# The front of an encoder trunk as one list of steps: no low parts on GpSimd, six chunks of h made by ScalarE, early transposes of the identity

## The chip, the cores and the metric

The kernel runs on one core of one Trainium2 chip. The metric is the time of one execution on the device, in microseconds (us). An execution has five engines that take their instructions in order and signal each other by semaphores: TensorE (PE, with its weight loads PEld), VectorE (DVE), ScalarE (ACT), GpSimd (POOL) and SyncE (SP, which here only issues transfers). The profile is of one profiled execution.

## The reference

One layer of a trunk over two inputs (prompt and sample, 512 rows of 1024 each). What matters here is its beginning, for the first input:

```python
c_act = jax.nn.silu(c)
mod = c_act @ w_ada[l] + b_ada[l]
sh1, sc1, g1, sh2, sc2, g2 = [m[:, None, :] for m in jnp.split(mod, N_MOD, axis=-1)]
h = rms_norm(x, norm1_g[l]) * (1.0 + sc1) + sh1
proj = h @ w_in[l]
q_a, k_a, v_a, q_r, k_r, v_r, g_r = jnp.split(proj, IN_OFFSETS, axis=-1)
```

Behind it come windowed attention on `q_a, k_a, v_a` (768 columns of `proj`), bidirectional retention on the rest, an output projection, a second norm and a squared-ReLU MLP, and a final norm. Everything is float32.

## The kernel before

**Products.** A float32 product is made of three matmuls of the type fp32r. Each operand is split in a high part (a cast, usually on ACT) and a low part (the value less its high part, a subtraction on DVE or POOL); `mm3` then adds high by high, high by low and low by high in one PSUM bank.

**The front.** The first 83 us work on the prompt alone. The 1024 inner columns are cut into eight chunks `kc` of 128. For each chunk the kernel needs: `xT[kc]`, the normed rows of x, transposed (`px`, PE, from four tiles of x that DVE has scaled by their own root mean square); a shift and a scale per column, `mod_s` and `mod_a`, from 128 columns of `w_ada` each; `hm = xT*a + s` (L326, DVE), its high part (L327, ACT) and low part (L328, DVE); and 768 columns of `w_in` (`wi`), split in `wih` and `wil`. `products(kc, ...)` multiplies the chunk into six open banks, `first`, one for each 128 columns of k, v and the four pieces of q: 18 matmuls of 512 columns a chunk. When chunk 7 is through, the banks are read and the retention and attention stages start.

**The modulation.** Chunk 0 and 1 have their columns of `w_ada` loaded alone (`one`: two halves of the 1024 rows, 512 bytes a run), the others by pairs of chunks (`pair`: for the scale, s=1, and the shift, s=0, two halves each of 512 KB). A pair's half is split (`wh_ada` on ACT, L97; `wl_ada` on DVE for half 0 and on POOL for half 1, L1002), 16 matmuls with the four columns `c4` give a row `pm`, ACT copies it out (`mr`, L221), two transposes turn it into columns (`pmt`, L229), and DVE adds their parts and finishes `mod` (L232, L234, L202, L204).

**What sets the order.** The front is written by hand as a program; `pin` makes every engine keep that order, up to chunk 6. Instructions of later stages are not pinned and may be put between pinned ones. Transfers that SP issues go one after another through one queue: where one waits for a buffer, all behind it wait. Raw tiles of `w_in` from chunk 2 on, and all later raw weights, share three buffers (`raw`); most other tiles share 32 buffers (`r4`). A raw tile's buffer comes free when its low part is made, which is on POOL for chunks 0 to 6 (L1025). The split parts of the chunks are also written to DRAM (`kept_first`, ACT's queue, L1048) for the second input, which reads them back around 207 to 250 us.

Of the kernel before, what the change touches and what calls it, by code (L numbers as in the profile page):

```python
# [15 lines left out]
P = 128  # L16
# [14 lines left out]
def trunk_kernel(ctx, tc, x0, x1, c0, c1, w_ada, b_ada, norm1_g, w_in, attn_sink, decay_f, decay_b,  # L31
# [123 lines left out]
    nc.gpsimd.dma_start(dec[:, 0, :], decay_f.broadcast_to([P, RH]))  # L155
    nc.gpsimd.dma_start(dec[:, 1, :], decay_b.broadcast_to([P, RH]))
    sink = const.tile([P, AH], F32, name="sink")
    nc.gpsimd.dma_start(sink, attn_sink.broadcast_to([P, AH]))
# [8 lines left out]

    def conditioning():
        ps = aux_bank("ps_rows")
        nc.tensor.transpose(ps[:, :80], rows, ident[:80, :80])  # L170
        nc.vector.tensor_copy(cols, ps[:, :80])
        th = small([P, 16], "cth")
        nc.scalar.activation(th, cols[:, 0:16], AF.Tanh, scale=0.5)
        yield
        nc.vector.scalar_tensor_tensor(cact.rearrange("p k b -> p b k"), th.rearrange("p (b k) -> p b k", b=NB), 1.0,
                                       cols[:, 0:16].rearrange("p (b k) -> p b k", b=NB), ALU.add, ALU.mult)
        nc.vector.tensor_scalar(cact, cact, 0.5, None, ALU.mult)
        yield
        nc.vector.tensor_scalar(onep, bcol[:, KC:2 * KC], 1.0, None, ALU.add)
        nc.vector.tensor_copy(c4[:, :, 0:2], cact)  # L180
        nc.vector.tensor_sub(c4[:, :, 2:4], cact, f(c4[:, :, 0:2]))
        yield
# [23 lines left out]
    def ada_sums(name, ws, done, stops=(), paired=False):  # L206

        split = isinstance(ws[0], list)
        m = 4 if split else NB
        pm = aux_bank(f"pm_{name}")  # L210
        out = pm[:m, :256].rearrange("p (c n) -> p c n", c=2)
        for kk in range(KC):
            kh, k = divmod(kk, 4)
            sides = [(c4, w) for w in ws[kh]] if split else [(cact, ws[kh].rearrange("p (c k n) -> p c k n", c=2, n=P))]
            for s, (c_, w) in enumerate(sides):
                nc.tensor.matmul(out, c_[:, kk, :], w[:, :, k, :], start=(kk == 0 and s == 0),
                                 stop=(kk == KC - 1 and s == len(sides) - 1))
            if kk in stops:
                yield
        mr = small([4, 256], f"mr_{name}", tag="mr", bufs=2)  # L220
        nc.scalar.copy(mr[:m, :], pm[:m, :256])  # L221
        yield
        pt = aux_bank(f"pmt_{name}")
        for c in range(2):
            mc = mr[:m, c * P:(c + 1) * P]
            if paired:
                nc.tensor.matmul(pt[:, c * 2:c * 2 + 2], mc, pairing, start=True, stop=True)
            else:
                nc.tensor.transpose(pt[:, c * m:c * m + m], mc, ident[:m, :m])  # L229
        if split and not paired:  # L230
            m4 = small([P, 2, 4], f"m4_{name}")
            nc.vector.tensor_copy(m4.rearrange("p c s -> p (c s)"), pt[:, 0:8])  # L232
            ms = small([P, 2, 2], f"ms_{name}")
            nc.vector.tensor_tensor(ms, m4[:, :, 0:2], m4[:, :, 2:4], ALU.add)  # L234
        else:
            ms = pt[:, 0:4].rearrange("p (c b) -> p c b", c=2)
        for c in range(2):
            done(c, ms[:, c, :])
        yield
# [75 lines left out]
    def x_rstd(b, t, xt):  # L315
        ssq = small([P, 1], f"ssq_{b}_{t}")
        nc.scalar.activation(junk(f"jk_{b}_{t}"), xt, AF.Square, accum_out=ssq)
        return rms_rstd(ssq, f"x_{b}_{t}")
# [184 lines left out]
    def masked_distance():  # L503
        nc.vector.tensor_scalar(sink8, sink, 8.0, None, ALU.mult)
        di = r4f("di")
        da, dm = di[:, :384], di[:, 384:768]
        nc.vector.scalar_tensor_tensor(da, dl[:, 256:640], -1.0, dl[:, 256:640], ALU.mult, ALU.max)
        nc.vector.tensor_scalar(dm, da, 128.5, MASKED, ALU.is_gt, ALU.mult)
        nc.vector.tensor_tensor(da, da, dm, ALU.add)
        return da  # L510

    def bias_tables(da):
        for h in range(AH):
            nc.scalar.activation(bias_t[:, h, :], da, AF.Copy, scale=-8.0 * 2.0 ** -(h + 1))
            yield
# [5 lines left out]
    def log_decays():  # L521
        decf = dec.rearrange("p a h -> p (a h)")
# [451 lines left out]
    xt0 += [load_x_tile(0, t) for t in range(2, NT)]  # L974
    wi, pairs = {}, {}

    def load_wi(kc):
        wi[kc] = raw_unit(cols_unit(w_in, kc, 1, 0, 768), f"wi_{kc}", spare=kc < 2)

    def load_one(kc):  # L980
        one = []
        for kh in range(2):
            t = r4f(f"raw_ada1_{kc}_{kh}")
            for s in range(2):
                in_order(nc.sync.dma_start(t[:, s * 512:(s + 1) * 512].rearrange("p (k n) -> p k n", n=P),
                                           cols_unit(w_ada, kh * 4, 4, s * D + kc * P, P)))
            one.append(t)
        return one

    def load_pair(kc):  # L990
        for s in (1, 0):
            for kh in range(2):
                pairs[kc, s, kh] = raw_unit(cols_unit(w_ada, kh * 4, 4, s * D + kc * P, 256), f"ada1_{kc}_{s}_{kh}", True)

    def high_pair(kc, s):
        for kh in range(2):
            t = pairs[kc, s, kh]
            pairs[kc, s, kh] = t, split_high(t, f"ada1_{kc}_{s}_{kh}", spare_ws if s == 0 else None)

    def low_pair(kc, s, kh, engine):  # L1000
        t, w = pairs[kc, s, kh]
        engine.tensor_sub(w[1], t, f(w[0]))  # L1002
        pairs[kc, s, kh] = [x.rearrange("p (k c n) -> p c k n", k=4, c=2) for x in w]

    def high_one(kc, kh):
        ones[kc][kh] = ones[kc][kh], split_high(ones[kc][kh], f"ada1_{kc}_{kh}", spare_ws)

    def low_one(kc, kh, engine):
        t, w = ones[kc][kh]
        engine.tensor_sub(w[1], t, f(w[0]))  # L1010
        ones[kc][kh] = [x.rearrange("p (c k n) -> p c k n", c=2, n=P) for x in w]

    def one(kc, **kw):
        return ada_sums(f"{kc}", ones[kc], lambda c, m: first_mod(c == 1, kc, m), **kw)

    def pair(kc, s):
        return ada_sums(f"{kc}_{s}", [pairs[kc, s, kh] for kh in range(2)], lambda c, m: first_mod(s == 1, kc + c, m))

    def split_wi(kc, engine=nc.vector, low=nc.gpsimd):
        w = [r4(f"wi{s}_{kc}").rearrange("p a n -> p (a n)")[:, :768] for s in "hl"]  # L1020
        if engine is nc.scalar:
            nc.scalar.copy(w[0], wi[kc][:, :768])
        else:
            nc.vector.tensor_copy(w[0], wi[kc][:, :768])
        low.tensor_sub(w[1], wi[kc][:, :768], f(w[0]))  # L1025
        wi[kc] = w

    def take_xT(kc, pt):
        if kc % 2 == 0:
            pair = r4(f"xT_{kc}", F32)  # L1030
            xT.extend([pair[:, 0, :], pair[:, 1, :]])
        if kc % 2 == 0:
            nc.scalar.copy(xT[kc], pt)
        else:
            nc.vector.tensor_copy(xT[kc], pt)

    def prepare(kc):
        hT[0].append(modulated(0, 0, kc, xT[kc]))

    def products(kc, c0, c1):  # L1040
        w, h_ = wi[kc], hT[0][kc]
        for c in range(c0, c1):
            cs = slice(order[c] * P, (order[c] + 1) * P)
            mm3(open_banks[c], (w[0][:, cs], w[1][:, cs]), (h_[:, 0, :], h_[:, 1, :]), kc == 0, kc == KC - 1)
        if c1 == 6:
            for k in ([] if kc == 0 else [kc - 1] if kc < KC - 1 else [kc - 1, kc]):
                for s in range(2):
                    nc.scalar.dma_start(kept_first[:, :, s, k * P:(k + 1) * P],  # L1048
                                        f(wi[k][s]).rearrange("p (c n) -> p c n", n=P))
# [43 lines left out]
    for kc in range(4):  # L1093
        take_xT(kc, banks[kc])
# [409 lines left out]
```

## Time and profile before

| what | us |
|---|---|
| median of 3 runs | 1155.02 (1154.34 to 1156.5) |
| the profiled execution | 1155.35 |
| its span in the trace | 1153.5 |
| first matmul of `products` starts | 24.21 |
| last matmul of `products` starts | 82.54 |
| PE busy in the span | 1108.4 (96%) |
| DVE, ACT, POOL busy | 899.6, 497.6, 68.2 |

The span is the time between the first and the last instruction that the trace shows; the profiled execution's own time is 1.85 us longer. A row of the timeline has the start, the duration, the engine, the line, the operation and its tiles, and in brackets the idle time of the engine just before it and what ended that. A row of the windows has busy time and number of instructions for each engine in a stretch, the clock granted to TensorE as a share, the mean busy share of the 16 DMA engines (it can be above 1, where packets overlap) and the rate of transfer.

### The profile page before, as it was taken

How to read it: one execution, taken by the hardware profiler on the slowest of the kernel's cores; microseconds unless marked ns; L12 is line 12 of the kernel's file. 1: busy time of each engine (PE TensorE's matmuls, PEld its weight loads, DVE VectorE, ACT ScalarE, POOL GpSimd, SP SyncE). 2: the span in 40 equal slices, each digit the busy share in tenths (PEclk: the TensorE clock that was granted, in tenths of full speed). 3: DMA queues.
4: the chain of work that ended last, by engine and by line, in shares of the span. 5: the costliest groups of instructions: out<-in, count | busy, mean ns of one | idle time of the engine just before them, and what ended most of it. 6: DMA issues, size and time to landing. Idle time of an engine off the chain costs nothing.

```text
span 1153.5 us, 14407 instructions
## 1 busy us (share of the span) xinstructions
PE 1108.4 (96%) x5167; PEld 903.5 (78%) x5167; DVE 899.6 (78%) x1496; ACT 497.6 (43%) x847; POOL 68.2 (6%) x79
## 2 busy tenths in 40 slices
PE   5989999999999999998999999999989999999995
PEld 3668787778888878887888888888778888888884
DVE  4888988978888687699998778876659655679675
ACT  4446765435554243355333333333434542335341
POOL 3620001100000000000000000000000000000011
PEclk9999999999999999999999999999999999999999
DMA  9786677665454689950655455442793455625503
GB/s 287 243 268 223 206 233 265 221 204 172 160 178 159 194 282 325 351 185 26 210 195 179 161 169 177 170 162 103 258 356 99 147 190 183 226 84 183 183 19 145
DMA packets 125135, 224.36 MB, mean 194 GB/s; under 512 B 8500, under 2 KB 59780, under 8 KB 125064
## 3 DMA queue, kind: packets, MB, share of 16 engines
q1 hardware_dynamic: 112168, 217.14, 55.9%
q10 hardware_dynamic: 12544, 6.29, 1.9%
q8 instruction: 40, 0.66, 0.2%
q0 software_dynamic: 352, 0.03, 0.2%
q14 instruction: 31, 0.25, 0.1%
HBM read 152.36 MB, written 71.06 MB: 194 GB/s over the span
## 4 chain that ended last, share of the span: by engine, by line
PE 78%; DVE 9%; DMA 7%; ACT 2%; issue 2%; POOL 1%; POOLq 0%; SPq 0%; ACTq 0%; DVEq 0%
PE x L1326 13%; PE px_None L937 12%; PE y L1326 11%; PE py_None L937 9%; PE po L129 2%; PE po L130 2%; PE po L128 2%; PE po L429 1%; PE ppt L422 1%; PE psc L396 1%; PE pj_rv L128 1%; PE pj_rv L130 1%; PE pj_rv L129 1%; PE pj_rg L130 1%; PE pj_rg L128 1%
## 5 line engine op out<-in xcount | busy, mean ns | idle before, releaser
L843 DVE TENSOR_TENSOR uc_l<-ur,uc_h 128x1024 fp32r<-128x1024 f32 x56 | 68.3, 1221 | 48.2 <-ACT uc_h L842 31.2
L1326 PE MATMUL x<-wc_h,uc_h 128*128 128x512 f32 x256 | 99.9, 391 | 4.4 <-DVE acc L1367 3.7
L1326 PE MATMUL x<-wc_l,uc_h 128*128 128x512 f32 x256 | 99.7, 390 | 0.0
L1326 PE MATMUL x<-wc_h,uc_l 128*128 128x512 f32 x256 | 99.7, 389 | 0.0
L842 ACT CAST uc_h<-ur 128x1024 fp32r<-128x1024 f32 x56 | 58.8, 1050 | 74.4 <-PE x L1326 22.7
L1326 PE MATMUL y<-wc_l,uc_h 128*128 128x512 f32 x192 | 75.6, 394 | 3.5 <-DVE wc_l L843 3.5
L1326 PE MATMUL y<-wc_h,uc_l 128*128 128x512 f32 x192 | 75.3, 392 | 0.0
L1326 PE MATMUL y<-wc_h,uc_h 128*128 128x512 f32 x192 | 75.2, 392 | 0.0
L842 ACT CAST wc_h<-w 128x1024 fp32r<-128x1024 f32 x48 | 50.4, 1050 | 49.9 <-PE x L1326 19.4
L843 DVE TENSOR_TENSOR wc_l<-w,wc_h 128x1024 fp32r<-128x1024 f32 x48 | 58.5, 1219 | 6.5 <-ACT wc_h L842 4.5
L1326 PEld LDWEIGHTS x<-wc_h,uc_h 128*128 128x128 f32 x256 | 48.1, 188 | 15.6 <-DVE acc L1367 4.5
L1326 PEld LDWEIGHTS x<-wc_h,uc_l 128*128 128x128 f32 x256 | 48.1, 188 | 10.0
L1326 PEld LDWEIGHTS x<-wc_l,uc_h 128*128 128x128 f32 x256 | 48.1, 188 | 9.9
L128 PE MATMUL po<-wh_wo,ms 128*128 128x512 f32 x128 | 50.5, 397 | 1.9 <-ACT ms L761 1.9
L129 PE MATMUL po<-wl_wo,ms 128*128 128x512 f32 x128 | 49.8, 391 | 0.3 <-DVE wl_wo L103 0.3
L130 PE MATMUL po<-wh_wo,ms 128*128 128x512 f32 x128 | 49.7, 391 | 0.0
L255 DVE SCALAR_TENSOR_TENSOR adacc_c<-raw_ada_c,cact,adacc_c 128x512 f32<-128x512 f32 x56 | 39.8, 746 | 8.6 <-DMA raw_ada_c<-in_w_ada_dram 7.6
L1326 PEld LDWEIGHTS y<-wc_l,uc_h 128*128 128x128 f32 x192 | 36.4, 190 | 11.6 <-DVE wc_l L843 4.0
L842 ACT CAST wc_s4h<-raw_w 128x1024 fp32r<-128x1024 f32 x16 | 16.9, 1054 | 62.6 <-PE px_None L937 41.6
L406 ACT ACTIVATE st<-st,negm 128x256 f32<-128x256 f32 (+1 forms) x64 | 35.2, 555 | 19.4 <-DVE negm L401 19.4
L1326 PEld LDWEIGHTS y<-wc_h,uc_l 128*128 128x128 f32 x192 | 36.5, 190 | 7.5
L1326 PEld LDWEIGHTS y<-wc_h,uc_h 128*128 128x128 f32 x192 | 36.4, 189 | 7.6
(380 smaller groups left out, 3083.3 us busy)
## 6 DMA issues: line engine op xcount, KB each, us to landing
ur<-spill SPq DMA_DIRECT2D x56, 512.0 KB, 4.1
raw_w<-in_w_mlp_dram SPq DMA_DIRECT2D x32, 512.0 KB, 3.9
spill<-s SPq DMA_DIRECT2D x64, 256.0 KB, 3.7
w<-in_w_mlp_dram SPq DMA_DIRECT2D x32, 512.0 KB, 7.0
spill<-u SPq DMA_DIRECT2D x48, 256.0 KB, 2.0
raw_ada_g<-in_w_ada_dram SPq DMA_DIRECT2D x16, 512.0 KB, 4.6
raw_ada_c<-in_w_ada_dram SPq DMA_DIRECT2D x16, 512.0 KB, 4.0
raw_ada<-in_w_ada_dram SPq DMA_DIRECT2D x12, 512.0 KB, 8.8
```

The source lines that it names most:

```text
L128: nc.tensor.matmul(ps, lhs[0], rhs[0], start=start, stop=False)
L129: nc.tensor.matmul(ps, lhs[0], rhs[1], start=False, stop=False)
L130: nc.tensor.matmul(ps, lhs[1], rhs[0], start=False, stop=stop)
L255: nc.vector.scalar_tensor_tensor(acc[b], src, cb, acc[b], ALU.mult, ALU.add)
L396: nc.tensor.matmul(psc[:, :w], qs[hh][:, isl], k_[:, s, j0 * P:j1 * P], start=(s == 0), stop=(s == 1))
L406: nc.scalar.activation(st[hh][:, :w], st[hh][:, :w], AF.Exp, bias=negm[:, hh:hh + 1], scale=0.125, accum_out=den[:, hh:hh + 1])
L422: nc.tensor.transpose(pt[:, hh * P:(hh + 1) * P], st[hh][:, jj * P:(jj + 1) * P], ident)
L429: nc.tensor.matmul(po, va[:, j0 + jj, g].rearrange("p s e -> p (s e)"), pts[jj][:, s, :], start=(jj == 0 and s == 0), stop=(jj == nj - 1 a ...
L842: nc.scalar.copy(hi, src)
L843: nc.vector.tensor_sub(lo, src, f(hi))
L937: self.last = nc.tensor.matmul(bank[:, cs], x[:, k, :], y, start=first and k == 0 and i == 0, stop=last and k == 3 and i == 2, skip_group_ ...
L1326: nc.tensor.matmul(out, left[n][x][:, i, ts_], right[n][y][:, i, :], start=first and i == 0 and k == 0, stop=end and i == 1 and k == 2, sk ...
```

## The change

The whole front becomes a list of short steps, `FRONT`, that is run in order; each step issues one piece of work (`P.2.0`: chunk 2 into bank 0; `pl.4.1.0`: the low part of pair 4, scale, half 0). `pin` again makes each engine keep the order of the list.

```diff
-    xt0 = [load_x_tile(0, t) for t in range(2)]
+    xt0 = {}
...
-        in_order(nc.sync.dma_start(rows[r0:r0 + n, :], src.rearrange("(r p) -> r p", p=P)))
+        in_order(nc.scalar.dma_start(rows[r0:r0 + n, :], src.rearrange("(r p) -> r p", p=P)))
...
+    BY_SCALAR = (0, 1, 2, 3, 5, 7)
+    kept_first = tc.dram_tile((P, KC, 2, 768), F32, name="kept_first")
+    for c in range(6):
+        kept[f"in{c * P}"] = kept_first.rearrange("p k s n -> p s k n")[:, :, :, c * P:(c + 1) * P]
...
+    def low(key, kh, form):
+        t, w = halves[key][kh]
+        nc.vector.tensor_sub(w[1], t, f(w[0]))
...
+    def step_wh(kc):
+        w = [r4(f"wi{s}_{kc}").rearrange("p a n -> p (a n)")[:, :768] for s in "hl"]
+        nc.scalar.copy(w[0], wi[kc][:, :768])
...
+    def step_wl(kc):
+        t, w = wi[kc]
+        nc.vector.tensor_sub(w[1], t[:, :768], f(w[0]))
...
+        if kc in BY_SCALAR:
+            nc.scalar.activation(d[:, 0, :], xT[kc], AF.Identity, bias=mod_s[0][:, kc, 0:1], scale=mod_a[0][:, kc, 0:1])
...
+    def step_keep(kc):
+        for s in range(2):
+            nc.gpsimd.dma_start(kept_first[:, kc, s, :], f(wi[kc][s]))
+
+    def step_warm(n):
+
+        b_ = aux_bank("warm")
+        for _ in range(n):
+            nc.tensor.transpose(b_[:, :P], ident, ident)
...
+    FRONT = """
+di.0 di.1 x.0 di.2 bias.0 bias.1 x.1 bias.2 bias.3 warm.12 psr warm.14 bias.4 cols one.0.0.0 bias.5 tanh sq.0
...
+wh.6 pm.p61.0 wh.7 pl.6.0.1 pm.p61.1 wl.6 pm.p60.0 mr.p61 wl.7 pt.p61 pm.p60.1 md.p61 P.3.5 keep.3
```

In words: all low parts are on DVE, all high parts of `w_in` on ACT. ACT makes `hm` and the high part of h for chunks 0, 1, 2, 3, 5 and 7, both straight from `xT`. The row `pm` and its columns share one bank, and a matmul with `pairing` (a 4x2 matrix of ones and zeros) adds the parts, so that DVE's copy and addition (L232, L234) go for every pair. 26 transposes of the identity stand on PE ahead of the first transposes of x. The bias tables of the attention (`bias`, ACT) are made at the start instead of among the chunks. The small loads of the conditioning (`rows`) go through ACT's queue, those of the retention (`dec`, `sink`) stand behind the front's first tiles on POOL, and the writes to `kept_first` go through POOL's queue, in runs of 3 KB instead of 512 bytes; the second input then reads them in runs of 512 bytes instead of 4 KB.

The order of SP's transfers at the start, before (x are the tiles of x, `raw_ada_0` the columns of chunk 0; two rows of one half are one tile):

```order
L146 DMA x_0_84<-in_x_prompt_dram 128x1024
L146 DMA x_1_86<-in_x_prompt_dram 128x1024
L153 DMA rows<-in_c_prompt_dram 8x128
L153 DMA rows<-in_c_sample_dram 8x128
L153 DMA rows<-in_norm_g_dram 8x128 x2
L153 DMA rows<-in_b_ada_dram 48x128
L146 DMA x_2_119<-in_x_prompt_dram 128x1024
L146 DMA x_3_121<-in_x_prompt_dram 128x1024
L985 DMA raw_ada_0_0_124<-in_w_ada_dram 128x4x128 x2
L985 DMA raw_ada_0_1_127<-in_w_ada_dram 128x4x128 x2
L89 DMA raw_wi_130<-in_w_in_dram 128x768
```

The same place after the change:

```order
L147 DMA x_0_116<-in_x_prompt_dram 128x1024
L147 DMA x_1_121<-in_x_prompt_dram 128x1024
L984 DMA raw_ada_0_0_157<-in_w_ada_dram 128x4x128 x2
L984 DMA raw_ada_0_1_171<-in_w_ada_dram 128x4x128 x2
L147 DMA x_2_183<-in_x_prompt_dram 128x1024
L147 DMA x_3_206<-in_x_prompt_dram 128x1024
L984 DMA raw_ada_1_0_219<-in_w_ada_dram 128x4x128 x2
L89 DMA raw_wi_242<-in_w_in_dram 128x768
```

Chunk 0's columns of `w_ada` come before the third and fourth tile of x, and the five small loads have left the queue. The rest of the queue up to the retention's first weights keeps its order.

POOL in the front, before, behind the last tile of x (`wil` and `wl_ada` are the low parts):

```order
L306 TENSOR_TENSOR rr_x_3_208<-rv_x_3_206,neghalf 128x1
L1025 TENSOR_TENSOR wil_241<-raw_wi_130,wih_240 128x768
L1025 TENSOR_TENSOR wil_287<-raw_wi_138,wih_286 128x768
L1002 TENSOR_TENSOR wl_ada_2_1_1_294<-raw_ada_2_1_1_142,wh_ada_2_1_1_293 128x1024
L1002 TENSOR_TENSOR wl_ada_2_0_1_341<-raw_ada_2_0_1_146,wh_ada_2_0_1_340 128x1024
L1025 TENSOR_TENSOR wil_358<-raw_wi_148,wih_357 128x768
```

And after:

```order
L1024 TENSOR_TENSOR rr_x_3_264<-rv_x_3_262,neghalf 128x1
L159 DMA dec<-in_ret_decay_fwd_dram 128x4
L160 DMA dec<-in_ret_decay_bwd_dram 128x4
L161 DMA sink<-in_attn_sink_dram 128x8
L1101 DMA kept_first<-wih_269 128x768
L1101 DMA kept_first<-wil_270 128x768
L1101 DMA kept_first<-wih_338 128x768
```

Thirteen subtractions have gone from POOL; what it has in their place is three small loads and sixteen writes, each issued as soon as its own chunk is split, since nothing else stands ahead of them on POOL.

ACT near the end of the front, before (`mr_1_665` and `mr_0_711` are the rows of pair 6, `wh_rv` the high part of the retention's first weights, not pinned):

```order
L221 COPY mr_1_665<-pm_1_648 4x256
L514 ACTIVATE bias_t<-di 128x384
L1048 DMA kept_first<-wih_449 768x1x128
L1048 DMA kept_first<-wil_450 768x1x128
L1048 DMA kept_first<-wil_595 768x1x128
L221 COPY mr_0_711<-pm_0_694 4x256
L514 ACTIVATE bias_t<-di 128x384
L1048 DMA kept_first<-wih_683 768x1x128
L327 CAST h_0_6_726<-hm_0_6_727 128x512
L1048 DMA kept_first<-wil_684 768x1x128
L97 CAST wh_rv_0_845<-raw_rv_0_843 128x1024
```

And after (`mr_p_664` and `mr_p_684` are the rows of pair 6, `wih_630` and `wih_642` the high parts of chunks 6 and 7):

```order
L97 CAST wh_ada_6_0_1_623<-raw_ada_6_0_1_556 128x1024
L1060 CAST wih_630<-raw_wi_576 128x768
L1060 CAST wih_642<-raw_wi_586 128x768
L97 CAST wh_rv_0_841<-raw_rv_0_839 128x1024
L210 COPY mr_p_664<-pm_p_633 4x256
L210 COPY mr_p_684<-pm_p_655 4x256
L522 ACTIVATE lg_z<-lg_ax 128x8
L1084 ACTIVATE h_0_7_704<-xT_376,mod_s_98,mod_a_96 128x512
L1086 CAST h_0_6_693<-hm_0_6_694 128x512
```

The high parts of the last two chunks and of the retention's first weights now stand ahead of both rows of pair 6. On PE the matmul that waits for the first of these rows (`pt.p61` in the list) stands ahead of the second half of the shift's sum, of the last product of chunk 3 and of all of chunks 4 to 7.

More of the change, by code (lines that the diff above doesn't have):

```diff
@@ L166, in trunk_kernel @@
     onep = const.tile([P, KC], F32, name="onep")
[L168 to L182, printed above, removed]
     mod_a = [const.tile([P, KC, NB], F32, name=f"mod_a{i}") for i in range(2)]
@@ L230, in ada_sums @@
[L230 to L236, printed above, removed]
-        for c in range(2):
-            done(c, ms[:, c, :])
-        yield
+            out, mc = bank_[:, 256 + c * 2:258 + c * 2], mr[key][:m, c * P:(c + 1) * P]
@@ L990, in load_pair @@
[L990 to L1017, printed above, removed]
@@ L1037, in prepare @@
[L1037 to L1049, printed above, removed]
@@ L1179, in trunk_kernel @@
-    next(tables)
-    pin(start)
-    products(KC - 2, 0, 6)
-    for c in range(6):
-        products(KC - 1, c, c + 1)
-        first[c].done(open_banks[c])
+    wi, halves, sums, mr, hm, xT, banks, open_banks, ssx, rrx = {}, {}, {}, {}, {}, {}, {}, {}, {}, {}
+    order = (4, 5, 0, 1, 2, 3)
+    BY_SCALAR = (0, 1, 2, 3, 5, 7)
+    kept_first = tc.dram_tile((P, KC, 2, 768), F32, name="kept_first")
+    for c in range(6):
+        kept[f"in{c * P}"] = kept_first.rearrange("p k s n -> p s k n")[:, :, :, c * P:(c + 1) * P]
@@ new lines, in trunk_kernel @@
+P.6.4 P.6.5 keep.6 P.7.0 P.7.1 P.7.2 P.7.3 P.7.4 P.7.5 keep.7
+    """.split()
+    start = len(nc.cur_bb.bb.instructions)
+    hT_of[0].extend([None] * KC)
+    first = attn_units(hT_of[0], 0)
+    for name in FRONT:
+        kind, *args = name.split(".")
+        if name == "P.7.0":
+            pin(start)
+        steps[kind](*[int(a) if a.isdigit() else a for a in args])
+        if kind == "P" and args[0] == "7":
+            first[int(args[1])].done(open_banks[int(args[1])])
+    hT = hT_of
```

346 lines of the change are left out of this document (159 added, 187 removed).

## Prediction

> **What bounds the kernel now.** The page first, for the whole; then the windows, by stage of the front.
>
> ```profile
> PE 1108.4 (96%) x5167; PEld 903.5 (78%) x5167; DVE 899.6 (78%) x1496; ACT 497.6 (43%) x847; POOL 68.2 (6%) x79
> ```
> ```profile
> 20.30:31.40 11.10, 10.88 (x54) 6.18 (x53) 7.41 (x16) 5.06 (x9) 3.85 (x3) 1.00 1.09 358
> 31.40:37.30 5.90, 3.77 (x28) 2.29 (x27) 5.88 (x4) 4.01 (x5) 3.88 (x2) 1.00 0.64 214
> 37.30:41.40 4.10, 4.10 (x18) 2.52 (x17) 4.05 (x3) 0.79 (x2) 4.07 (x2) 0.58 0.27 67
> 41.40:60.60 19.20, 17.92 (x94) 12.97 (x93) 15.37 (x29) 7.43 (x12) 9.30 (x6) 1.00 0.76 240
> 60.60:72.00 11.40, 9.22 (x57) 6.45 (x56) 9.49 (x18) 4.51 (x8) 5.92 (x3) 1.00 0.95 273
> 72.00:83.20 11.20, 11.20 (x47) 8.34 (x46) 8.57 (x22) 5.96 (x10) 0.00 (x0) 1.00 0.97 300
> ```
>
> PE is busy nearly all the time; behind 72 us it has no gap at all, so a front that ends sooner moves everything behind it. In the front the transfers carry 358 GB/s until 31.4 us, then fall to 67 while PE waits and its clock drops to 0.58. The queue's own waits say why, and the timeline of DVE and POOL why that took so long:
>
> ```profile
> SPq L89 <- POOL wil L1025: 27.2, 4, 9.2
> ```
> ```profile
> 33.34 3.39 DVE L1002 TENSOR_TENSOR wl_ada<-raw_ada,wh_ada 128x1024 fp32r<-128x1024 f32 x1
> ```
> ```profile
> 33.24 2.41 POOL L1002 TENSOR_TENSOR wl_ada<-raw_ada,wh_ada 128x1024 fp32r<-128x1024 f32 x1 [0.37 <-ACT wh_ada L97]
> ```
>
> SP stood 27.2 us for buffers that POOL's low parts release, and a DVE subtraction that takes 1.22 us elsewhere (below) took 3.39 with POOL's beside it. The front's marks on PE, and the pitch of its matmuls:
>
> ```profile
> 24.21 0.50 PE L128 MATMUL first<-h,wih 128*128 128x512 f32 x1
> 46.01 0.28 PE L216 MATMUL pm<-wh_ada,c 128*4 128x256 f32 x1
> 47.85 0.40 PE L128 MATMUL first<-h,wih 128*128 128x512 f32 x1
> 66.08 0.28 PE L229 MATMUL pmt<-ident,mr 4*128 4x4 f32 x2 [2.10 <-ACT mr L221]
> 66.29 0.50 PE L128 MATMUL first<-h,wih 128*128 128x512 f32 x1
> 82.31 0.39 PE L129 MATMUL first<-h,wih 128*128 128x512 f32 x1
> 82.54 0.39 PE L130 MATMUL first<-h,wil 128*128 128x512 f32 x1
> ```
>
> A product matmul starts every 0.23 us (82.31 to 82.54), so a product of three takes 0.69, a pair's 16 sums take 1.84 (46.01 to 47.85), two column matmuls 0.21 (66.08 to 66.29). The front ends at 82.54 + 0.23 = 82.8.
>
> **The change, part by part.**
>
> *Low parts to DVE.* What the move costs and frees, from the groups by form:
>
> ```profile
> L1002 DVE TENSOR_TENSOR wl_ada<-raw_ada,wh_ada 128x1024 fp32r<-128x1024 f32 x6 | 9.5, 1582 | 0.9 <-ACT wh_ada L97 0.9
> L328 DVE TENSOR_TENSOR h<-hm,h 128x512 fp32r<-128x512 f32 x8 | 9.2, 1151 | 5.5 <-ACT h L327 5.5
> L202 DVE TENSOR_SCALAR mod_a<-ms,onep,cols 128x2 f32<-128x2 f32 x6 | 5.0, 871 | 0.1
> L234 DVE TENSOR_TENSOR ms<-m 128x4 f32<-128x4 f32 x6 | 4.3, 716 | 0.2
> L1024 DVE CAST wih<-raw_wi 128x768 fp32r<-128x768 f32 x7 | 3.9, 551 | 0.0
> L1010 DVE TENSOR_TENSOR wl_ada<-raw_ada,wh_ada 128x1024 fp32r<-128x1024 f32 x2 | 2.4, 1223 | 0.0
> L1025 DVE TENSOR_TENSOR wil<-raw_wi,wih 128x768 fp32r<-128x768 f32 x1 | 1.0, 959 | 0.0
> L97 ACT CAST wh_rv<-raw_rv 128x1024 fp32r<-128x1024 f32 x2 | 2.1, 1050 | 0.0
> L221 ACT COPY mr<-pm 4x256 f32<-4x256 f32 x7 | 2.5, 360 | 12.2 <-PE pm L216 12.2
> ```
>
> DVE gains 6 x 1.22 + 7 x 0.96 = 14.0 us and loses the casts of w_in (3.9), the sums `ms` (4.3) and what POOL's neighbourhood added: 6 x (1.58 - 1.22) = 2.2 on `wl_ada`, 8 x (1.15 - 0.69) = 3.7 on h (0.69 is its duration in the undisturbed row quoted further down). So DVE has no more work than before, and 41.4 to 60.6 us shows 15.37 of 19.2. ACT gains seven casts and six second activations of about 0.6, some 9 us, over a front in which it was idle half the time. Neither becomes the bound.
>
> *The start.* Before, the fourth tile of x and the row of chunk 0 came one after the other:
>
> ```profile
> 13.02 1.06 ACT L317 ACTIVATE jk<-x 128x1024 bf16<-128x1024 f32 x1 [0.18 <-DMA x<-in_x_prompt_dram]
> ```
> ```profile
> 22.96 0.55 DVE L326 TENSOR_SCALAR hm<-xT,mod_a,mod_s 128x512 f32<-128x512 f32 x1
> ```
>
> Now the columns of chunk 0 land ahead of the last tiles, so `hm` waits for x alone. The tile's squares, root, scaling, transposes and two copies are about 6 us behind its landing; with the bytes ahead unchanged (12 to 13 us) the first product starts near 20 instead of 24.2. The eight bias tables now stand ahead of the first tiles' squares and put these off by some 2 us; the wait for the fourth tile hides that, and without it those 2 us would be the price. The identity transposes lie on PE in the same wait: nothing. The small loads of `dec` and `sink` are needed only behind chunk 6, some 40 us after POOL issues them: nothing.
>
> *Transfers.* POOL no longer holds SP, so what lands when goes by bytes. The waits for low parts stay: the raw tile of chunk 5 needs the low part of chunk 2, which lands 2.9 MB ahead of it, so 8 us or more at 350 GB/s, against some 2 us for its split. If DVE fell behind by 6 us, SP would stand again. These are the transfers of the window up to 83 us, the issue of the first write on ACT's queue, and the rates in 40 slices of 2.08 us:
>
> ```profile
> raw_ada<-in_w_ada_dram SPq DMA_DIRECT2D x12, 512.0 KB, 8.8
> raw_wi<-in_w_in_dram SPq DMA_DIRECT2D x8, 384.0 KB, 5.8
> kept_first<-wih ACTq DMA_DIRECT2D x8, 384.0 KB, 4.6
> kept_first<-wil ACTq DMA_DIRECT2D x8, 384.0 KB, 6.0
> x<-in_x_prompt_dram SPq DMA_DIRECT2D x4, 512.0 KB, 4.4
> raw_ada<-in_w_ada_dram SPq DMA_DIRECT2D x8, 256.0 KB, 6.1
> ```
> ```profile
> 46.11 0.57 ACTq L1048 DMA_DIRECT2D kept_first<-wih  x1
> ```
> ```profile
> GB/s 30 316 178 135 359 339 217 348 300 352 349 348 374 372 349 350 280 24 0 154 354 326 343 311 284 262 133 184 0 106 127 338 346 346 315 185 380 350 375 218
> ```
>
> Reads to the end of the front: 2.10 (x) + 8.39 (w_ada) + 3.15 (w_in) = 13.6 MB, and 0.52 for the retention's first weights. The first of the writes (6.3 MB) began at 46 us; now each goes out when its chunk is split, from about 18 us, into the same engines. For chunks 0 to 5 that is 12 x 0.393 = 4.7 MB ahead of the last reads: 18.9 MB. Rates are bounded by the windows, 300 (72 to 83.2) and 358 (20.3 to 31.4); I take 345, the full slices' usual figure. The flow begins near 3 us (0.52 MB had landed at 4.3, the next row), so the last read lands at 3 + 18.9/0.345 = 57.8 us; bounds 55.8 and 66.
>
> ```profile
> 4.32 1.06 ACT L317 ACTIVATE jk<-x 128x1024 bf16<-128x1024 f32 x1 [2.32 <-DMA x<-in_x_prompt_dram]
> ```
>
> *The new wait at the end.* ACT's order has `wih` of chunks 6 and 7 and `wh_rv` ahead of the rows of pair 6; all three wait for those last reads, and PE's column matmul behind the row holds all products left. From 57.8: `wh_rv` 1.05, row 0.36, columns 0.21, half a sum 0.92, one product 0.69, second row and columns 0.57, 24 products x 0.69 = 16.6. Sum 20.4: the front ends at 78.2. PE would wait some 3 us there; the earlier gap brought the clock to 0.58 for 4.1 us, so (1 - 0.58) x 4.1 = 1.7 us may be added; the gap of 2.10 at 66 us cost none. I take none and keep 1.7 for the range. The Trainium skill ("TensorE: Matmul & The Clock Gate", Part 1) has the clock fall after an idle window of about 3.4 us; by that a wait of 3 us costs nothing and the sum stays; by the row it could be 79.9. The first gap, 5.90 us with 3.77 busy, was shorter than that window and cost all the same, so the row decides for the range.
>
> *Reading back.* The second input now reads `kept_first` in 512-byte runs. `raw_rq`, in such runs, and `wh_q`, in long ones, both landed in
>
> ```profile
> DMA to landing us min/median/max: 4.9/4.9/4.9
> ```
>
> and the engines have room there, so I take 0; at worst 12 loads 15% slower than 1.5 us each, 2.7 us, if none were hidden.
>
> Sum: 78.2 - 82.8 = -4.6, so 1155.35 - 4.6 = 1150.75 for the profiled execution (span 1153.5 and the 1.85 around it, which stays); the median of the runs, 1155.02, is 0.3 below that execution. I say **1150.4**.
>
> **Rivals.**
> 1. *The writes do not hold the reads.* If they come late, 14.1 MB at 345 land by 44 us and PE is the bound: 20 + 144 x 0.23 + 6 x 1.84 + 6 x 0.21 = 65.4, with some gaps 65 to 67, gain 16, **1139**. For it: only reads are urgent. Against: POOL has nothing ahead of the writes. POOL's issue of a small write, and DVE beside it:
>
> ```profile
> 191.43 0.55 POOL L292 DMA_DIRECT2D gates<-adacc_g  x1 [6.33 <-ACT adacc_g L291]
> ```
> ```profile
> 191.73 0.68 DVE L328 TENSOR_TENSOR h<-hm,h 128x512 fp32r<-128x512 f32 x1
> ```
>
> Neither is longer than elsewhere. Yet the Trainium skill ("SBUF — State Buffer", SBUF: two separate sides) says that a transfer issued from GpSimd waits for its descriptors while DVE runs an operation that uses the shared port. By it the writes would be pushed back under a DVE that is 80% busy, which here leads to this rival; these rows do not show it.
>
> 2. *The engines are slower with reads and writes mixed* (slower than before). At 300 GB/s the last read lands at 66 us and the front ends at 86.4: +3.6, **1158.6**. The point from which it decides is 18.9/(82.8 - 20.4 - 3) = 318 GB/s. For it: 273 and 300 in the two windows that had reads and writes, and a slow start (178 and 135). Against: their slices hold holes, and full ones with both have 311 to 380; the writes' runs are six times longer.
> 3. *Nothing changes* (within 0.2%): the same place at 310 to 325 GB/s, or the clock's 1.7 us and some of the reading back on top: **1154**.
>
> **How the numbers follow.** Forecast (gain 2.5 to 10 us) 0.58; rival 1 and what lies toward it (more than 10) 0.12; rival 3 0.17; rival 2 0.13. A change of 0.2%, 2.3 us, is about what a measurement of this kernel can tell from none. So faster 0.70, same 0.17, slower 0.13. The range leaves out rival 1's far half and rival 2's: 1142 to 1157.
>
> **What would show it.** Right: POOL without subtractions, no DVE subtraction of 1024 above 1.3 us; first product near 20; transfers above 320 GB/s from 10 to 55 us, with writes from 18 us on; one long wait of PE for `mr` near 54 to 59; front's end near 78. Wrong: the wait at `mr` missing with an end below 72 (rival 1), the last reads landing after 62 (rival 2), or PE gaps behind the front that were not there.

## The result and the profile after

The changed kernel takes 1148.73 us (median of 7 runs, 1146.14 to 1149.94) against 1155.02 for the kernel before in the same rounds: ratio 0.9945, 95% interval 0.993 to 0.9959. The forecast was 1150.4, in 1142 to 1157. The profiled execution took 1147.91, its span is 1145.2: 7.4 us under the one before, and 8.3 in the span. (Of the experiments below, one execution of e6, of 3343.1 us, counts in its median but not in its ratio.) The first line of its page, with the busy time of each engine:

```profile
PE 1111.3 (97%) x5205; PEld 909.7 (79%) x5205; DVE 889.1 (78%) x1484; ACT 506.8 (44%) x860; POOL 46.8 (4%) x82
```

The windows of the front, cut as before, and one more piece of its start:

```profile
20.30:31.40 11.10, 11.10 (x63) 7.79 (x62) 9.26 (x13) 10.46 (x16) 1.08 (x2) 1.00 1.03 347
31.40:37.30 5.90, 4.01 (x27) 2.90 (x27) 4.48 (x6) 3.19 (x4) 2.15 (x4) 1.00 1.08 383
37.30:41.40 4.10, 4.10 (x30) 2.85 (x30) 1.74 (x4) 1.05 (x1) 0.00 (x0) 1.00 1.02 413
41.40:60.60 19.20, 16.78 (x97) 12.38 (x96) 15.23 (x24) 14.73 (x21) 4.34 (x8) 1.00 1.00 348
60.60:72.00 11.40, 11.40 (x52) 9.40 (x51) 6.49 (x24) 3.20 (x5) 0.00 (x0) 1.00 0.96 362
72.00:83.20 11.20, 10.88 (x54) 8.80 (x53) 7.42 (x12) 7.44 (x14) 0.00 (x0) 1.00 0.01 2
```
```profile
10.00:16.00 6.00, 5.27 (x26) 3.94 (x27) 4.64 (x8) 4.91 (x10) 1.10 (x2) 0.55 1.05 329
```

The hole in the transfers (67 GB/s at 37 to 41 us) is gone; from 20 us on they run at 347 to 413 GB/s until everything has landed. The clock is whole from 16 us on, but 0.55 from 10 to 16. Now PE's marks in its timeline (in brackets the wait just before), the last being the first product behind the front:

```profile
18.68 1.53 PE L1034 MATMUL px<-ident,x 128*128 128x128 f32 x12
20.14 1.89 PE L204 MATMUL pm_o<-raw_ada,cact 128*2 128x256 f32 x8
21.96 1.09 PE L301 MATMUL px<-ident,x 128*128 128x128 f32 x8
23.19 0.50 PE L129 MATMUL first<-h,wih 128*128 128x512 f32 x1
36.62 0.60 PE L217 MATMUL pm_p<-pairing,mr_p 4*128 4x2 f32 x4 [1.89 <-ACT mr_p L210]
42.77 0.28 PE L204 MATMUL pm_p<-wh_ada,c 128*4 128x256 f32 x1 [1.18 <-ACT wh_ada L97]
44.03 0.28 PE L204 MATMUL pm_p<-wl_ada,c 128*4 128x256 f32 x1 [0.98 <-DVE wl_ada L1055]
57.11 0.60 PE L217 MATMUL pm_p<-pairing,mr_p 4*128 4x2 f32 x4
76.38 0.39 PE L129 MATMUL pj_rv<-wh_rv,h 128*128 128x512 f32 x1
```

The front ends at 76.4 instead of 82.8. The long wait that was forecast at the row of pair 6 (57.11) is not there; the waits stand at pair 4, at 36.6 and at 42.8 to 44. ACT's timeline says what these waited for, and how close the forecast's place came:

```profile
41.67 1.04 ACT L97 CAST wh_ada<-raw_ada 128x1024 fp32r<-128x1024 f32 x1 [2.99 <-DMA raw_ada<-in_w_ada_dram]
55.74 1.05 ACT L97 CAST wh_rv<-raw_rv 128x1024 fp32r<-128x1024 f32 x1 [1.01 <-DMA raw_rv<-in_w_in_dram]
56.70 0.35 ACT L210 COPY mr_p<-pm_p 4x256 f32<-4x256 f32 x1
```

The last read that PE stands for is the last half of pair 4 (ACT has it at 41.67); from 44.03 on PE runs almost without a gap. The read of rv is in ACT's hands at 55.74, against 57.8 forecast, and the row leaves ACT at 57.05, when PE had just run dry. Groups of VectorE, SP's wait, and the writes' issue on POOL (0.54 us each; first, eighth and ninth):

```profile
L1055 DVE TENSOR_TENSOR wl_ada<-raw_ada,wh_ada 128x1024 fp32r<-128x1024 f32 x14 | 16.8, 1220 | 5.6 <-ACT wh_ada L97 5.6
L1090 DVE TENSOR_TENSOR h<-hm,h 128x512 fp32r<-128x512 f32 x8 | 5.4, 689 | 1.6 <-ACT h L1084 1.0 <-ACT h L1086 0.4 <-ACT hm L1077 0.2
```
```profile
SPq L89 <- DVE wil L1065: 6.0, 3, 3.8
```
```profile
18.59 0.54 POOL L1101 DMA_DIRECT2D kept_first<-wih  x1
34.42 0.54 POOL L1101 DMA_DIRECT2D kept_first<-wil  x1 [0.22 <-issue]
46.83 0.54 POOL L1101 DMA_DIRECT2D kept_first<-wih  x1 [11.87 <-ACT mr_p L210]
```

**Where the 6.4 us of the front come from.** From 9.4 us (before, the first transposes of x; now, the end of the early ones) to the first product of rv PE waited 8.5 us before and 5.7 now: 2.8. The other 3.6 lie in busy time: of 73.4 us 64.9 before, of 67.0 us 61.3 now. Before, the clock was half up to 20.3 us (the windows' 1.00 is no evidence there: the sums before stood 0.21 us apart, 17.93 to 18.14 in PE's timeline, and 0.12 from 20.4 on), over 8.2 us of work, which cost 4.1, and again for 3.4 us at 37.4, which cost 1.7; now it is half from 10.7 to 15.4 (sums 0.21 us apart up to 15.26, 0.11 from 15.44 on), which costs 2.3. 5.8 - 2.3 = 3.5. This divides PE's time; it does not show causes. In e1, e3, e5 and e6 below the clock is whole from about 11 us on, and the first product comes at 22.9 to 23.2 all the same, so those 2.3 us cost the first product 0.3 us at most; what the longer half clock cost the kernel before is not shown. Behind the front PE's waits up to 300 us fall from 4.1 to 1.7 us; two of those that went:

```profile
124.66 0.51 PE L130 MATMUL pj_rk<-h,wl_rk 128*128 128x512 f32 x1 [0.83 <-DVE wl_rk L103]
...
246.53 0.50 PE L130 MATMUL pj_q<-h,wl_q 128*128 128x512 f32 x1 [0.79 <-DMA wl_q<-kept_first]
```

Front and waits make 8.8 us; the span fell by 8.3. The rest of the way has gains and losses that the change did not aim at: some waits are shorter, and the same wait of 2.89 us near the end brought half clock (the matmul behind it takes 0.80 us) in this execution and none before. Here before, then after:

```profile
1127.79 0.50 PE L1326 MATMUL x<-wc_h,uc_h 128*128 128x512 f32 x1 [2.89 <-DVE acc L1367]
```
```profile
1117.96 0.80 PE L1291 MATMUL x<-wc_h,uc_h 128*128 128x512 f32 x1 [2.89 <-DVE acc L1332]
```

So the front's 6.4 us and the 6.3 us between the medians agree, but not because everything else stood still.

### The profile page after: what moved, and what is told of

It reads as the page before. It is cut to its first block, busy times and chain, and to the rows that moved or that the text cites. A ratio compares the mean times of both kernels' runs of the same rounds, so it can differ in the third digit from the quotient of the medians.

```text
span 1145.2 us, 14502 instructions
## 1 busy us (share of the span) xinstructions
PE 1111.3 (97%) x5205; PEld 909.7 (79%) x5205; DVE 889.1 (78%) x1484; ACT 506.8 (44%) x860; POOL 46.8 (4%) x82
## 4 chain that ended last, share of the span: by engine, by line
PE 81%; DVE 8%; DMA 6%; ACT 2%; issue 2%; POOL 1%; SPq 0%; ACTq 0%; POOLq 0%; DVEq 0%
PE x L1291 13%; PE px_None L933 12%; PE y L1291 12%; PE py_None L933 9%; PE po L130 2%; PE po L131 2%; PE po L129 2%; PE po L421 2%; PE ppt L414 2%; PE psc L388 1%; DMA raw_ada<-in_w_ada_dram 1%; PE pj_rv L129 1%; PE pj_rv L130 1%; PE pj_rv L131 1%; PE pj_rg L129 1%
## 5 line engine op out<-in xcount | busy, mean ns | idle before, releaser
L1291 PE MATMUL y<-wc_l,uc_h 128*128 128x512 f32 x192 | 76.1, 396 | 4.3 <-DVE wc_l L839 4.3
```

The lines of the kernel that those rows point to most:

```text
L1291: nc.tensor.matmul(out, left[n][x][:, i, ts_], right[n][y][:, i, :], start=first and i == 0 and k == 0, stop=end and i == 1 and k == 2, sk ...
```

## The experiments

Ratios are to the kernel before in the same rounds; "rv at" is the start of the first product behind the front in the profiled execution.

| run | edit | median us | ratio (95%) | rv at |
|---|---|---|---|---|
| before | | 1155.02 | 1 | 82.8 |
| after | the change | 1148.73 | 0.9945 (0.993 to 0.9959) | 76.4 |
| e1 | writes late, SP | 1150.36 | 0.9958 (0.9942 to 0.9974) | 75.2 |
| e2 | writes twice | 1159.71 | 1.0045 (1.0028 to 1.0062) | 90.0 |
| e3 | low parts on GpSimd | 1147.14 | 0.9936 (0.9919 to 0.9953) | 77.6 |
| e4 | before + low parts on DVE | 1164.59 | 1.0091 (1.0071 to 1.011) | 88.8 |
| e5 | list, old engines | 1151.13 | 0.9977 (0.996 to 0.9995) | 87.1 |
| e6 | list, all on DVE | 1152.37 | 0.9968 (0.9955 to 0.9982) | 79.6 |
| e7 | one early transpose | 1150.56 | 0.9958 (0.9944 to 0.9973) | 80.0 |
| e8 | writes held | 1151.78 | 0.997 (0.9958 to 0.9982) | 81.8 |
| e9 | rv behind the rows | 1148.28 | 0.9944 (0.9925 to 0.9963) | 76.8 |
| e10 | e8 and e9 | 1144.18 | 0.9912 (0.9888 to 0.9937) | 72.6 |
| e11 | old layout | 1150.52 | 0.9964 (0.9951 to 0.9977) | 77.1 |
| e12 | before + ACT's share | 1158.81 | 1.0032 (1.0019 to 1.0046) | 86.8 |

### Do the writes hold the reads? e1, e2

```diff
 def step_keep(kc):
-            nc.gpsimd.dma_start(kept_first[:, kc, s, :], f(wi[kc][s]))
+            nc.sync.dma_start(kept_first[:, kc, s, :], f(wi[kc][s]))
```

> The sixteen writes to the kept tensor go through SP's queue, behind the last raw tile of the front, so none of them runs beside the reads up to about 44 us. Theory A (bytes set the front: the reads of pair 4 land late because 3.1 MB of writes share the engines with them): the last half of pair 4 lands about 8 us earlier than 41.7, the waits of PE at 34.7, 41.6 and 43.1 us (4.1 us in all) go, the first product of rv starts at 72.2 instead of 76.4, and the time is 4 us under that of the change: ratio to before about 0.991. Theory B (writes do not hold reads): the waits stay, 76.4, ratio 0.9945.

The last product of the front started at 71.3 and the waits at 34.7 to 44 were gone, as theory A has it. The time did not follow. Timelines of ACT and PE, and a window:

```profile
74.12 1.05 ACT L97 CAST wh_rv<-raw_rv 128x1024 fp32r<-128x1024 f32 x1
```
```profile
74.39 0.50 PE L388 MATMUL psc<-ks,qs 128*128 128x256 f32 x2 [2.24 <-DVE qs L366]
```
```profile
75.30:85.60 10.30, 9.28 (x22) 6.59 (x23) 8.35 (x19) 5.42 (x14) 0.00 (x0) 0.50 0.71 253
```

The weights of rv came behind the writes on SP, so ACT's order had their split behind the heads' queries (74.12 instead of 55.74), PE had nothing to put into the queries' wait, and the clock stood at half for the 10.3 us after it: some 5 us, all that the front had won. It was the place and not the transfer: the reads were issued from 56.3 us on and landed 5.9 us after their issue, while ACT was idle from 58.3 to 68.4.

```diff
+    kept_again = tc.dram_tile((P, KC, 2, 768), F32, name="kept_again")
...
             nc.gpsimd.dma_start(kept_first[:, kc, s, :], f(wi[kc][s]))
+            nc.gpsimd.dma_start(kept_again[:, kc, s, :], f(wi[kc][s]))
```

> Every write of the front is made a second time, to a tensor that nobody reads: 6.3 MB more, on the same queue. Theory A: 3.1 MB more stand ahead of the last half of pair 4, at 375 GB/s 8.4 us, so the first product of rv starts near 84.8 and the time is 8 us above that of the change: ratio to before about 1.002. Theory B: nothing moves, 76.4, ratio 0.9945.

Slower by 11.0 us than the change; theory A in direction, and 5 us more than it said (90.0 against 84.8). PE's waits show the surplus:

```profile
62.18 0.28 PE L204 MATMUL pm_p<-wh_ada,c 128*4 128x256 f32 x1 [3.28 <-ACT wh_ada L97]
...
68.74 0.58 PE L217 MATMUL pm_p<-pairing,mr_p 4*128 4x2 f32 x2 [3.64 <-ACT mr_p L210]
```

The second is the forecast's wait at the row of pair 6, which here is real, and the forecast's working goes on from it: 68.74, 19.0 (its 20.4 less the split and the row, which are done by then) and 2.3 for the half clock up to 73.3 make 90.0. Theory B falls: writes do hold reads.

### Which engines bring it? e3, e4, e5, e6, e12

```diff
 def low(key, kh, form):
-        nc.vector.tensor_sub(w[1], t, f(w[0]))
+        (nc.gpsimd if key[0] == "p" and kh == 1 else nc.vector).tensor_sub(w[1], t, f(w[0]))
...
 def step_wl(kc):
-        nc.vector.tensor_sub(w[1], t[:, :768], f(w[0]))
+        (nc.gpsimd if kc < 7 else nc.vector).tensor_sub(w[1], t[:, :768], f(w[0]))
```

(In `FRONT`, each `keep.k` moved behind its `wl.k`.)

> The change with the same thirteen low parts as before back on GpSimd, each chunk's writes right behind its low part. Theory A (GpSimd's low parts were what held the transfers): SP waits for them again, a stretch under 150 GB/s comes back between 30 and 45 us, and the first product of rv starts at 81 or later, ratio 0.998 to 1.002. Theory C (the gain is the clock at the start and the new order): the first product of rv stays below 78.5, ratio 0.996 or less.

As fast as the change. SP's wait and two windows:

```profile
SPq L89 <- POOL wil L1065: 24.5, 4, 10.9
```
```profile
31.40:37.30 5.90, 5.55 (x35) 3.96 (x34) 4.55 (x5) 5.42 (x7) 5.88 (x5) 1.00 0.99 321
37.30:41.40 4.10, 1.83 (x13) 1.06 (x13) 3.99 (x4) 3.17 (x5) 4.08 (x5) 1.00 1.01 384
```

SP stands for POOL almost as long as in the kernel before (24.5 against 27.2 us), but the writes, which now go out early, keep the engines full meanwhile. Theory A falls: the longest wait in SP's list was not what the time hung on.

```diff
-    def split_wi(kc, engine=nc.vector, low=nc.gpsimd):
+    def split_wi(kc, engine=nc.vector, low=nc.vector):
...
-    low_pair(2, 1, 1, nc.gpsimd)
+    low_pair(2, 1, 1, nc.vector)
```

(and so at the other four calls, and for chunk 5.)

> The kernel before, with nothing changed but the thirteen low parts, which VectorE makes. Theory A: SP's wait of 27 us goes, the first product of rv starts 4 us or more earlier than 82.8, ratio 0.996 or less. Theory D (VectorE, which here still makes h, the sums of the rows and the high parts, falls behind by the 14 us that it is given): the front ends no earlier than 82, ratio 0.999 or more.

9.7 us slower than before: theory D. SP now waits for VectorE, and PE for rows and copies that are late by it:

```profile
SPq L89 <- DVE ms L234: 8.3, 1, 8.3
```
```profile
67.31 0.37 PE L229 MATMUL pmt<-ident,mr 4*128 4x4 f32 x2 [3.87 <-ACT mr L221]
...
88.75 0.50 PE L128 MATMUL pj_rv<-wh_rv,h 128*128 128x512 f32 x1 [3.10 <-ACT vt_a L353]
```

So the part of the change that stands first in its description costs 0.9% by itself, in the old order. The next two put the list under other engines, both with

```diff
-    BY_SCALAR = (0, 1, 2, 3, 5, 7)
+    BY_SCALAR = ()
...
 def step_wh(kc):
-        nc.scalar.copy(w[0], wi[kc][:, :768])
+        (nc.scalar.copy if kc == 0 else nc.vector.tensor_copy)(w[0], wi[kc][:, :768])
```

the first on top of e3's edit (and with `hm` always made ahead of `hh`):

> The change's list of steps with the engines of before: low parts on GpSimd as in the third run, h and its chunks by VectorE with one cast on ACT, the high parts of w_in on VectorE (chunk 0 on ACT). Theory O (the order of the steps in the queues brings the gain, the engines little): the first product of rv starts below 78.5 and the ratio to before is 0.994 to 0.996. Theory S (ACT's share of h and w_in is what pays): the first product of rv starts at 81 or later, ratio 0.998 or more.

> The same, but with the low parts on VectorE as in the change: it has now the low parts, h and the high parts of w_in, some 7 us more than in the change. Theory O: VectorE, busy 56 of 76 us in the change's front, has room for it, the first product of rv stays below 79, ratio 0.996 or less. Theory S (VectorE becomes the bound, as in the kernel before with its low parts on VectorE): 82 or later, ratio 1.000 or more.

The four cases of the list form a square:

| ratio | low parts on GpSimd | low parts on VectorE |
|---|---|---|
| h and w_in's high parts on VectorE | e5 0.9977 | e6 0.9968 |
| on ACT | e3 0.9936 | after 0.9945 |

Read across: where the low parts are made makes no difference that these runs can tell. Read down: ACT's share is worth 0.41% in the left column, whose intervals lie apart, and 0.23% in the right, where they touch. Both theories were half right: the list alone is worth 0.2 to 0.3%, ACT's share within it 0.2 to 0.4%. e5's profile is of one of three long executions out of twelve (1158.3; the rest lie at 1150.0 to 1152.1), so its 87.1 is not typical; it shows what such an execution waits for, GpSimd's low part of pair 4, with half a clock later on:

```profile
43.72 0.28 PE L204 MATMUL pm_p<-wl_ada,c 128*4 128x256 f32 x1 [3.54 <-POOL wl_ada L1055]
```

e6's one large wait is the forecast's, at the row of pair 6:

```profile
56.24 1.01 PE L217 MATMUL pm_p<-pairing,mr_p 4*128 4x2 f32 x4 [3.59 <-ACT mr_p L210]
```

Then ACT's share alone, in the old order:

```diff
-    def split_wi(kc, engine=nc.vector, low=nc.gpsimd):
+    def split_wi(kc, engine=nc.scalar, low=nc.gpsimd):
...
 def prepare(kc):
+        if kc not in (0, 1, 2, 3, 5, 7):
...
+        for d in (t, dst[:, 0, :]):
+            nc.scalar.activation(d, xT[kc], AF.Identity, bias=mod_s[0][:, kc, 0:1], scale=mod_a[0][:, kc, 0:1])
```

> The kernel before, with nothing changed but ACT's share: the high parts of w_in and both activations of h for chunks 0, 1, 2, 3, 5 and 7 on ACT, low parts on GpSimd as they were. In the list this share is worth 4 us (the third run against the fifth). Theory S (it is worth as much in any order): the first product of rv starts at 79 to 80, ratio 0.9955 to 0.9975. Theory L (it pays only where the list gives it its places; in the old order ACT's casts, which wait for reads, stand ahead of rows that PE waits for): 82 or later, ratio 0.999 or more.

Slower by 0.32%: theory L, though not at the place it named. The last product of the front started at 79.4, 3.1 us earlier than before; the loss came behind it, as in e1, where PE waited for the heads' queries with no product of rv ready:

```profile
82.49 0.50 PE L396 MATMUL psc<-ks,qs 128*128 128x256 f32 x2 [2.25 <-DVE qs L374]
85.11 1.90 PE L396 MATMUL psc<-ks,qs 128*128 128x256 f32 x6 [2.12 <-DVE qs L374]
```

### The early transposes: e7

```diff
 def step_warm(n):
-        for _ in range(n):
+        for _ in range(1):
```

> Each of the two groups of early transposes of the identity is cut to one. Theory E (the clock rises with the work on x itself, whatever went before): the first product stays at 23.2 and the front's end at 76.4, ratio 0.9945. Theory W (they raise the clock): the work from 10.7 us on runs up to 2.3 us longer, the first product starts up to 2.3 us later; the wait of 1.9 us at 34.7 us hides most of that, ratio 0.9945 to 0.996.

```profile
10.86 3.03 PE L1034 MATMUL px<-ident,x 128*128 128x128 f32 x12 [3.02 <-DVE rv_x L1020]
...
59.19 0.60 PE L217 MATMUL pm_p<-pairing,mr_p 4*128 4x2 f32 x4 [2.39 <-ACT mr_p L210]
```

The twelve transposes of x take 3.03 us without them and 3.02 with them (10.73 in the change's timeline), the half clock's pace in both; the first product comes at 23.37 against 23.19. That is theory E, but for these two executions alone. In e1, e3, e5 and e6, which have all 26, the transposes of x run faster, six in 0.88 us where the kernel before took 1.49 for six. From e3's timeline:

```profile
11.44 0.88 PE L1034 MATMUL px<-ident,x 128*128 128x128 f32 x6 [0.25 <-DVE rv_x L1020]
12.92 0.88 PE L1034 MATMUL px<-ident,x 128*128 128x128 f32 x6 [0.61 <-DVE x L313]
```

So the early transposes can raise the clock, as theory W has it, and did not in every execution. It brings next to nothing, because PE then waits for VectorE: e3's first product comes at 22.96. The ratio of e7 is 0.13% higher with the intervals overlapping, and its profile has the wait at pair 6, which the early transposes cannot reach; whether they are worth a microsecond in other executions stays open.

### The row behind the read: e8, e9, e10

```diff
+    def step_hold(key, kh):
+        nc.gpsimd.tensor_copy(small([1, 1], f"hold_{key}"), f(halves[key][kh][1][0])[0:1, 0:1])
...
-... pm.p41.0 ph.4.0.1 md.p20 ...
+... pm.p41.0 ph.4.0.1 hold.p40.1 md.p20 ...
```

> The writes stay on GpSimd's queue, but a copy of one element of the last high part of pair 4 stands ahead of them on GpSimd, so that they begin when pair 4 has landed (about 34 us instead of 18.6), and SP's queue stays as it is. Theory A: pair 4 lands some 8 us earlier, the three waits of PE at 34.7 to 44 us go, and since the weights of rv no longer stand behind the writes as in the first run nothing is lost behind the front: the first product of rv at 72.3 to 73.5, 3 to 4 us under the change, ratio 0.991 to 0.992. Theory N (the wait only moves to the row of pair 6, whose reads now share the engines with the writes): 75.5 or later, ratio 0.994 or more.

Theory N: 3 us slower than the change. ACT, PE and the window behind:

```profile
56.95 1.04 ACT L97 CAST wh_rv<-raw_rv 128x1024 fp32r<-128x1024 f32 x1 [3.66 <-DMA raw_rv<-in_w_in_dram]
```
```profile
58.31 1.01 PE L217 MATMUL pm_p<-pairing,mr_p 4*128 4x2 f32 x4 [6.42 <-ACT mr_p L210]
```
```profile
54.00:67.70 13.70, 9.39 (x29) 7.03 (x30) 5.29 (x20) 4.75 (x8) 1.29 (x3) 0.50 0.99 401
```

The waits at pair 4 are gone (PE has none of 0.3 us between 16 and 51), and all of it comes back at the row of pair 6, with a half clock of 13.7 us on top. Is it the row's own reads, or the split of rv ahead of it on ACT? e9 and e10 move that split alone, on the change and on e8 (`front_end` holds ACT's and VectorE's last instruction up to `hl.7`):

```diff
 def split_unit(src, name, lo_engine, pool=None):
+        n0 = len(nc.cur_bb.bb.instructions)
         w = split_high(t, name, pool)
         lo_engine.tensor_sub(w[1], t, f(w[0]))
+        if name in ("rv0_0", "rv0_1"):
+            for i in list(nc.cur_bb.bb.instructions)[n0:]:
+                if i.engine in front_end:
+                    tc.add_manual_dep(i, front_end[i.engine].name, mybir.DependencyInfo(
+                        mybir.DependencyClass.NoSync, mybir.DependencyReason.DATA), reason="order")
```

> The change, with the first two splits of rv put behind the front's own work on ACT and VectorE, so that the rows of pair 6 no longer stand behind the read of rv. Theory M (that queue place costs the change 2 to 4 us in part of its executions, by a wait like the 2.39 us of the seventh run and the half clock behind it): the executions lie closer together and the median falls by 1 to 3 us, ratio to before 0.991 to 0.9935. Theory Z (the read comes in time, as the change's profile shows with 0.1 us): ratio 0.9945, first product of rv at 76.3.

> The eighth run (writes held until pair 4 has landed) with the same new place of rv's splits. Theory A with M: the 6.42 us wait at the row of pair 6 and the half clock of 13.65 us behind it go, PE has no wait above 0.6 us between 16 and 72 us, the first product of rv starts at 72.3 to 73.5, and the time is 3 to 4 us under the change: ratio 0.989 to 0.9915. If something else held that row (pair 6's own reads, which share the engines with the writes): a wait above 1 us stays there, 75 or later, ratio 0.994 or more.

e9 is the change again (theory Z): where the read of rv comes in time, its place costs nothing. In e10 the wait and the half clock are gone:

```profile
53.34 0.60 PE L223 MATMUL pm_p<-pairing,mr_p 4*128 4x2 f32 x4 [0.62 <-ACT mr_p L216]
...
72.61 0.39 PE L135 MATMUL pj_rv<-wh_rv,h 128*128 128x512 f32 x1
```
```profile
54.00:67.70 13.70, 13.70 (x66) 11.07 (x65) 8.55 (x30) 4.50 (x7) 1.84 (x3) 1.00 1.02 417
```

72.6 as expected, and 1144.18 us: 0.88% under before, and by the ratios 0.33%, 3.8 us, under the change (the two intervals overlap by 0.07%). It is the best version of these runs. Neither edit gains without the other.

### The layout: e11

```diff
-    kept_first = tc.dram_tile((P, KC, 2, 768), F32, name="kept_first")
+    kept_first = tc.dram_tile((P, 6, 2, 1024), F32, name="kept_first")
...
-            nc.gpsimd.dma_start(kept_first[:, kc, s, :], f(wi[kc][s]))
+            nc.gpsimd.dma_start(kept_first[:, :, s, kc * P:(kc + 1) * P], f(wi[kc][s]).rearrange("p (c n) -> p c n", n=P))
```

> The change with the kept tensor laid out as before: the writes go in runs of 512 bytes, the second input reads it in runs of 4 KB. Theory A: the shorter runs hold the engines longer, pair 4 lands 1 to 4 us later and the first product of rv starts at 77.5 to 80.5; the reading back gains nothing, since PE does not wait for it in the change. Ratio 0.995 to 0.998. Theory F (the length of a run does not matter to the front): 76.4, ratio 0.9945 or, if reading back mattered, less.

rv at 77.1, 0.7 us later, below theory A's range; the ratio is 0.19% higher with intervals that overlap. So writes in runs of 3 KB instead of 512 bytes are worth 0.7 us to the front by these two profiles, 0 to 2 us to the whole, and no gain from reading back in long runs shows.

## Why the prediction held, step by step

- **Transfers as the bound of the front.** Right in kind: e2 against the change and e10 against e9 move the front's end with the writes, by +13.6 and -4.2 us. Right in bytes: up to 55.74 us the trace has 14.2 MB on SP's queue (the reads) and 19.1 MB in all, against the sum's 18.9. The rate was low at the start (302 GB/s from 16 to 23.2 us, under the 320 that was named as a sign) and then 347 to 413, not 345, so the read of rv landed two microseconds earlier than the sum had it. Wrong in the read that PE stood for: it is the last half of pair 4, behind eight writes (POOL's issues up to 34.4 us), not the last read of all, behind twelve.
- **The new wait at the end.** Forecast as 3 us; 0.1 us in the change's profile, where it is a near miss. It is there in e2 (3.64), e6 (3.59), e7 (2.39) and e8 (6.42), and e10 shows by removing it that ACT's order makes it. With the read's measured time the forecast's sum stands: 55.74 + 20.4 = 76.1, against 76.4. But PE had already stood 4.1 us at pair 4, which the forecast did not see, and reached the row at the same time as the read did. That the two meet within 0.1 us is luck: e9 takes the read out of the row's way, and the front ends at 76.8 all the same.
- **The first product near 20.** Failed: 23.2. The working followed x alone and gave it 6 us from the tile's landing; from ACT's squares of that tile, which began at 13.77 without a wait for it, it took 9.4. PE's own order has three microseconds of other work between 20.14 and the product (the marks above), VectorE finished h at 23.1, and the clock was half until 15.4. It cost nothing, since PE had no gap from 13.4 to 34.7.
- **Low parts to DVE.** The costs were right (1.22 us each, h back at 0.69), the role was not. That POOL "no longer holds SP" was given as what frees the reads; e3 lets POOL hold SP for 24.5 us and loses nothing, and e4 gives the move alone, in the old order, and loses 0.9%.
- **ACT's nine microseconds "neither becomes the bound".** True, but they were entered as a cost that hides, while in the list they are part of the gain: 0.41% of 0.64% (e3 against e5) or 0.23% of 0.55% (the change against e6).
- **The clock.** The forecast took no loss and kept 1.7 us. Of the 6.4 us in the front, 3.5 are busy time at a clock that was half before and is not now. The forecast's sum, which goes by the reads, had no term for that; how much of it moved the front's end is not shown.
- **Reading back at 0**: held (e11, and no wait of PE there). **Rival 1** (writes do not hold reads, POOL's pushed back under a busy DVE) fell by e2; POOL's issues took 0.54 us each (one 0.57) beside a DVE that was busy 15.2 of 19.2 us. That is no sign of the rule of the Trainium skill ("SBUF — State Buffer", SBUF: two separate sides) from which this rival had part of its chance, the wait of GpSimd's transfers under VectorE's work on the shared port. It is no full test either: the page names one kind of VectorE's operations, and no row here tells which ones were of it. **Rival 2** (a mixed rate under 318) fell by the windows.

So the sign and most of the size came out of a byte count whose end was right to 2 us, and which met the end of PE's own work by luck, while the reason given for the earlier reads, POOL's lost subtractions, was not the cause. What in the list brings its 0.2 to 0.3% (the start, the row's columns, the writes off ACT) was not taken apart and stays open.

## What to carry to other kernels

A long wait of a queue is a bound only if nothing else can use what it leaves free: move the waiting thing alone (e3, e4) before building on it. In an order written by hand, look for an instruction that waits for a distant read and stands ahead of a short one that PE needs at once; it costs nothing until some other change makes the read late, and then it costs the wait and the clock behind it. A gain in one stage is kept only if the next stage's first products are ready to fill its waits (e1, e12).

## What the hardware showed

The price of a wait of PE is not its length. A wait of 1.77 us (before, at 35) brought 3.4 us of half clock, 1.89 (after, at 34.7) and 2.10 (before, at 64) none, 2.39 (e7) 3.4, 3.59 (e6) 10.2, 3.87 (e4, at 63) 3.4, 4.80 (e2, at 31) 3.4, 6.42 (e8) 13.7, always in steps of 3.4 us. The Trainium skill ("TensorE: Matmul & The Clock Gate", Part 1) has a free-running window of about 3.4 us and a clock that falls after an idle one: the steps agree, but here the clock fell after waits of half a window, and in e8 stayed half for 9.4 us of unbroken work behind the wait (58.3 to 67.7).

The 26 early transposes of the change end at 9.35 us, 1.4 us before the first transposes of x, and the granted clock is 0.55 from 10 to 16 all the same. In e3 they end at 11.2, 0.25 us before x, and x runs at the faster pace. A warm-up with a gap behind it can be lost, and even where it holds the first product may wait for something else (22.96 against 23.19).
